# Sums over partitions as one marked float32 product, and page numbers read early, in a decoder-layer step

## The chip, the cores and the metric

The kernel runs on one core of a Trainium2 chip. The metric is the device time of one execution in microseconds; the number quoted for the kernel before is the median of three runs. One further execution was profiled, and all rows shown come from it.

## The reference

One layer of a decoder is applied to a prompt of 256 tokens and to eight samples of four tokens each, with the same float32 weights. Cut to what matters here:

```python
h = rms_norm(x, g_mix)
proj = h @ w_in                              # conv, q/k/v, memory q, three gates
u = u_lin * sigmoid(u_gate)                  # conv branch: causal depthwise conv, width 31
c = silu(layer_norm(depthwise(u), g_conv_ln, b_conv_ln));  y_conv = c @ w_conv_out
q = rms_norm(q_sb, g_q_sb);  k = rms_norm(k_sb, g_k_sb)    # 8 heads of 128
z = q . k / sqrt(128) + b_sb                 # stick-breaking attention, strictly causal
log_keep = where(causal, log_sigmoid(-z), 0)
after = reverse_cumsum(log_keep) - log_keep  # sum over the keys between s and t
a = where(causal, exp(log_sigmoid(z) + after), 0);  y_sb = (a @ v) @ w_sb_out
y_mem = softmax(rms_norm(q_mem) . k_mem / sqrt(128)) @ v_mem @ w_mem_out   # 256 memory tokens, 4 heads
x = x + (gA * y_conv + gB * y_sb + gM * y_mem) @ w_o
x = x + square(relu(rms_norm(x, g_mlp) @ w_up)) @ w_down
```

The samples also attend to a paged cache of 256 past tokens: `page_table` (8 samples x 2 pages) says which pages of `cache_sb_k` and `cache_sb_v` are theirs. New keys, values, convolution states and memory keys and values are outputs too.

## The kernel before

Activations lie with features on the 128 partitions and the 288 tokens (256 of the prompt, 32 of the samples) along the free dimension. All weights come from one array `wall` of 504 slabs of 128 x 1024 float32 (512 KB), in the order of their use; four slabs fit in the buffers `wr`.

Precision of the large products is kept by splitting. A cast on ScalarE (`cast_weights`, line 295) writes the part of a slab that the format float32r holds, `wh`; a subtraction on VectorE (`sub_part`, line 306) writes the rest, `wl`, and frees the slab buffer for the next load (line 278). Activations are split likewise into `h` and `l`. Each weight block of 128 x 128 then takes three products of 288 columns (`chunk`, line 465): high with high, high with low, low with high. A slab of eight blocks is 24 products.

Sums over the 128 partitions (of squares in the norms) are products with a matrix of ones. `total` (lines 429 and 430) makes them from an operand that was split first, with `ones_r`, a float32r copy of the ones: two products of 288 columns. It is called by `sum_norm` for the two norms over the model dimension, twice by `conv_norm`, and once in each of the 20 `head_norm`s (8 keys, 8 queries, 4 memory queries). In each stick-breaking head (`sb_head`) the sum over later keys is a product with a triangular matrix of zeros and ones: two products of 384 columns with `tri_r` (lines 1072 and 1074) on a split operand, and between them one of 128 columns with `ones` in plain float32 (line 1073). `mem_norm` (line 455) sums the memory's squares with four plain float32 products of one column. Other small products, such as scores (lines 843 and 1050) and transposes (lines 852 and 1036), are plain float32.

The order of instructions on each engine is written out at build time by the class `Order`. Each step of the work is a generator that yields `Ask(engine, us, flags, ...)`; the planner gives every step a price, keeps a clock for each engine and for the buffers, and places the step whose planned start comes first, with a rank for ties. Engines then run their queues in that order, waiting on semaphores. `MM` and `MM_MEM` are planned prices of products. The planner's `SP` is the SyncE queue, which issues nearly every transfer: slabs, `xT` and `memT`, stores, and tiles of the caches (`load_tiles`, nine buffers `k4`).

The 16 page numbers are loaded into `pt` early by one small transfer and read into SyncE registers inside `page_tiles` (line 927), when the first tile of cached keys is asked for; after that each tile is issued as two transfers (line 931). The planner counts 0.9 us for each tile and nothing more for the first. The four stages that use page tiles are the cached keys and then values of heads 0 to 3, and the same for heads 4 to 7; two stages before them use the memory caches through the same `load_tiles`.

In `sb_head`, after a head's value projection is scaled on VectorE (line 1031), PE transposes it (line 1036), and at the end of a head ScalarE and VectorE split its output (lines 1092 and 1094).

Of the kernel before, what the change touches and what calls it, by code (L numbers as in the profile page):

```python
# [7 lines left out]
F32 = mybir.dt.float32  # L8
# [6 lines left out]
P = 128  # L15
# [3 lines left out]
NB = 8  # L19
# [154 lines left out]
VISIT = 4  # L174
MM = 0.1325
MM_MEM = 0.226


@with_exitstack
def tile_decoder_step(ctx: ExitStack, tc: tile.TileContext, xT, memT, wall, cvec, kmat, ptab,  # L180
# [46 lines left out]
    nc.gpsimd.memset(eps, EPS)  # L227
    ones = cpool.tile([P, P], F32, name="ones")
    nc.gpsimd.memset(ones, 1.0)
    ones_r = cpool.tile([P, P], F32R, name="ones_r")  # L230
    nc.vector.tensor_copy(ones_r, ones)
# [10 lines left out]
    tri_r = cpool.tile([P, P], F32R, name="tri_r")  # L242
# [9 lines left out]

    def col(c):
        return cv[:, c:c + 1]

    def blocks2(x, n):

# [115 lines left out]
    def loads():  # L373

        xs = [(0, 3), (3, 6), (6, 9), (9, 12), (12, 15), (15, 16)]
        for k2 in range(KT // 2):
            yield sp(s=1)
            raw = tl("s", [P, 512]).rearrange("p (k t) -> p k t", k=2)
            here = [Flag(), Flag()]
            for i in range(2):  # L380
                if i:
                    yield sp()
                nc.sync.dma_start(raw[:, i], memT[:, 2 * k2 + i, :])
                here[i].at = order.landed(131)
                for s in (2 * k2, 2 * k2 + 1):
                    yield sp(**({} if i else {"wr": 1}))
                    load_slab(s, i)
                if i == 0:
                    add(prep_mem(k2, raw, here), 0.5 + 0.01 * k2)
            if k2 >= 1 and xs:  # L390
                k0, k1 = xs.pop(0)
                yield sp(k4=1)
                x = tl("k4", [P, 1024])[:, :(k1 - k0) * T].rearrange("p (k t) -> p k t", k=k1 - k0)
                nc.sync.dma_start(x, xT[:, k0:k1, :])
                there = Flag()
                there.at = order.landed(147 * (k1 - k0))
                for k in range(k0, k1):
                    add(prep_x(k, x[:, k - k0], there, k == k1 - 1), 1.5 + 0.01 * k)
            if k2 == 1:
                yield sp()  # L400
                nc.sync.dma_start(cv[:, C_BGATE:], cvec[:, C_BGATE:])
            if k2 == 2:
                yield sp()
                nc.sync.dma_start(km, kmat)
                km_in.at = order.landed(213)
                yield sp()
                nc.sync.dma_start(pt, ptab)
        for s in range(KT, N_SLABS):
            yield sp(wr=1)
            load_slab(s, 0)  # L410
# [12 lines left out]
        yield dve(n)  # L423
        nc.vector.scalar_tensor_tensor(out, a, 1.5, y, op0=ALU.add, op1=ALU.mult)

    def total(h, l, n):

        ss = bank("pa")[:, :n]
        nc.tensor.matmul(ss, ones_r, h, start=True, stop=False)  # L429
        nc.tensor.matmul(ss, ones_r, l, start=False, stop=True)  # L430
        return ss

    def sum_norm(acc, dim, out, flag, ready):

        yield act(T, ready, t=2)
        acc = acc[0]
        h, l = tl("t", [P, T], F32R), tl("t", [P, T], F32R)
        nc.scalar.copy(h, acc)
        yield dve(T)
        nc.vector.tensor_sub(l, acc, h.bitcast(F32))  # L440
        yield pe(2 * MM, pa=1)
        ss = total(h, l, T)
        yield from rsqrt_of(ss, T, dim, acc, tl("t", [P, T]), out)
        give("pa")
        give("t", 3)
        done(flag)

    rm_done, rx_done, r2_done = Flag(), Flag(), Flag()

    def mem_norm():  # L450
        yield pe(1.0, sums_m, pa=1)
        ss = bank("pa")[:, :MT]
        for m in range(MT):
            for i in range(2):
                nc.tensor.matmul(ss[:, m:m + 1], mem_sum[0][:, i * ML + m * P:i * ML + (m + 1) * P], ones[:, 0:1],
                                 start=(i == 0), stop=(i == 1))
# [233 lines left out]
    def conv_norm():  # L690

        yield dve(T, *conv_done, t=1)
        acc = tl("t", [P, T])
        nc.vector.tensor_add(acc, conv[0], conv[1])
        for j in (2, 3):
            yield dve(T)
            nc.vector.tensor_add(acc, acc, conv[j])
        for turn in range(2):
            yield act(T, t=1)
            h = tl("t", [P, T], F32R)  # L700
            nc.scalar.copy(h, acc)
            yield dve(T, t=1)
            l = tl("t", [P, T], F32R)
            nc.vector.tensor_sub(l, acc, h.bitcast(F32))
            yield pe(2 * MM, pa=1)
            ss = total(h, l, T)
            give("t", 2)
# [65 lines left out]

    def head_norm(ps, gcol, box, flag, p="pm"):

        yield dve(T, rx_done, t=4)
        raw, sq, h, l = (tl("t", [P, T], F32R if i > 1 else F32) for i in range(4))
        nc.vector.tensor_mul(raw, ps, rx)
        give(p)
        yield act(T)  # L780
        nc.scalar.activation(sq, raw, AF.Square)
        yield act(T)
        nc.scalar.copy(h, sq)
        yield dve(T)
        nc.vector.tensor_sub(l, sq, h.bitcast(F32))
        yield pe(2 * MM, pa=1)
        ss = total(h, l, T)
# [6 lines left out]
        give("t", 4)  # L794
        box.append(out)
        done(flag)

# [109 lines left out]

    def load_tiles(load, tiles, flags, which):
        for b in which:
            yield Ask("SP", 0.9, (), k4=1)  # L910
            t, kb = load(b)
            tiles.append(t)
            flags[b].at = order.landed(kb) + 1.0
# [5 lines left out]
            return t, 524  # L919
        return load  # L920

    pages = []

    def page_tiles(cache, g, spec):
        def load(b):
            if not pages:
                pages.extend(nc.sync.value_load(pt[0:1, i:i + 1], min_val=0, max_val=kpool.shape[0] - 1)
                             for i in range(2 * NB))
# [98 lines left out]
    def sb_head(h):  # L1027
        def evac(ps):
# [15 lines left out]
            give("pa")  # L1044
            give("a")
            done(v_made[h])
            yield pe(0.75, k_made[h], q_made[h], pa=1, s=4)
# [5 lines left out]
            z, l, sp_, hh = (tl("s", [P, 512], F32R if i == 3 else F32) for i in range(4))  # L1053
# [10 lines left out]
            nc.scalar.copy(hh[:, :384], ss)  # L1064
# [4 lines left out]
            nc.vector.tensor_sub(low, ss, hh[:, :384].bitcast(F32))  # L1069
            yield pe(0.6, pa=1)  # L1070
            af = bank("pa")[:, :384]
            nc.tensor.matmul(af, tri_r, hh[:, :384], start=True, stop=False)
            nc.tensor.matmul(af[:, 128:256], ones, sp_[:, 256:384], start=False, stop=False)
            nc.tensor.matmul(af, tri_r, low, start=False, stop=True)
            yield dve(384)
            nc.vector.tensor_sub(zz, zz, af)
            give("pa")
            give("s", 3)
            yield act(384)
            act_fn(LN_EXP, zz, zz, AF.Exp)  # L1080
            yield dve(256)
# [268 lines left out]
            give("a", 32)  # L1350

    def setup():
        yield dve(P, km_in)
        nc.vector.tensor_copy(tri_r, tri)
        yield pool(1)
        nc.gpsimd.memset(sb_s[:, T:T + 1], 0.0)

    with tc.manual_schedule():
# [165 lines left out]
```

## Time and profile before

| | |
|---|---|
| runs | 1669.57, 1672.0, 1673.81 us; median 1672.0 |
| profiled execution | 1670.29 us, span from first to last instruction 1668.3 us |
| PE (TensorE products) | busy 1661.0 us, 12778 records |
| DVE (VectorE) | busy 960.2 us, 1401 instructions |
| ACT (ScalarE) | busy 731.4 us, 1035 instructions |
| POOL (GpSimd) | busy 137.6 us |
| weight slabs | 488 loads of 512 KB and 32 of 256 KB |
| cache pages | 64 loads of 256 KB |

PEld is PE's loading of weights, which overlaps its products. SPq is SyncE's queue. Names of tiles are those of the program: `wr`, `wh`, `wl` are a raw slab, its high and its low part; `pm`, `pa`, `pl` are PSUM banks; `a`, `t`, `s` are activation tiles; `k` is a tile of a cache; `km` holds the constant matrices. Lnnn is a line of the kernel; a product in plain float32 can stand in the trace as more than one record.

### The profile page before, as it was taken

To read this page: it belongs to the slowest core of one execution; us is meant where nothing else is said; L and a number is where in the kernel's file an instruction comes from. 1 tells how busy PE (TensorE), PEld (TensorE's weight loads), DVE (VectorE), ACT (ScalarE), POOL (GpSimd) and SP (SyncE) were. 2 spreads that over 40 slices of the span, in tenths; PEclk is the share of its full clock that TensorE was granted. 3 is DMA by queue.
4 is the path that set the end of the run, shared out by engine and by line. 5 is a ranking of instruction groups with operands and counts; after the bars stand their busy time and mean duration, and the time that the engine had idled before them with its cause. 6 is when DMAs were issued, how large, how long until landed. Compare 5 with 4: busy or idle time off the path is not lost.

```text
span 1668.3 us, 30827 instructions
## 1 busy us (share of the span) xinstructions
PE 1661.0 (100%) x12778; PEld 1640.9 (98%) x12778; DVE 960.2 (58%) x1401; ACT 731.4 (44%) x1035; POOL 137.6 (8%) x105
## 2 busy tenths in 40 slices
PE   9999999999999999999999999999999999999999
PEld 7999998999999999999999999999999999999999
DVE  7887877776765555555555544455444554445443
ACT  8746655553463334444443333333333333333332
POOL 0020000000000000001222200122001210022100
PEclk9999999999999999999999999999999999999999
DMA  9686557756554555556655555555555555555553
GB/s 329 215 181 235 201 198 258 270 201 229 169 164 163 168 165 166 165 166 193 191 174 166 165 165 168 166 168 168 166 165 166 165 169 170 165 164 165 176 188 98
DMA packets 107103, 305.38 MB, mean 183 GB/s; under 512 B 19923, under 2 KB 29523, under 8 KB 106963
## 3 DMA queue, kind: packets, MB, share of 16 engines
q1 hardware_dynamic: 106818, 303.39, 57.3%
q8 instruction: 100, 1.64, 0.4%
q14 instruction: 41, 0.33, 0.1%
q10 hardware_dynamic: 144, 0.02, 0.0%
HBM read 297.05 MB, written 6.32 MB: 182 GB/s over the span
## 4 chain that ended last, share of the span: by engine, by line
PE 98%; DMA 1%; ACT 0%; SPq 0%; DVE 0%; issue 0%; ACTq 0%
PE pm L465 91%; PE pm L516 3%; PE pa L465 1%; PE pl L952 1%; DMA wr<-in_wall 1%; PE pl L1112 0%; DMA k<-in_kpool 0%; PE pl L968 0%; PE pa L1050 0%; PE pa L843 0%; PE pa L860 0%; PE pa L430 0%; PE pa L429 0%; PE pa L852 0%; PE pa L1051 0%; ACT wh L295 0%
## 5 line engine op out<-in xcount | busy, mean ns | idle before, releaser
L465 PE MATMUL pm<-a,wh 128*128 128x288 f32 x7744 | 1115.8, 295 | 0.0
L465 PEld LDWEIGHTS pm<-a,wh 128*128 128x128 f32 x7744 | 1054.4, 188 | 1.6 <-issue 1.4
L295 ACT CAST wh<-wr 128x1024 fp32r<-128x1024 f32 (+1 forms) x520 | 530.3, 1023 | 680.7 <-PE pm L465 621.5
L306 DVE TENSOR_TENSOR wl<-wr,wh 128x1024 fp32r<-128x1024 f32 (+1 forms) x520 | 618.3, 1192 | 213.4 <-ACT wh L295 210.9
L465 PE MATMUL pm<-a,wl 128*128 128x288 f32 x3872 | 600.6, 295 | 0.0
L465 PEld LDWEIGHTS pm<-a,wl 128*128 128x128 f32 x3872 | 542.8, 188 | 0.8 <-issue 0.6
L1249 POOL TENSOR_TENSOR t<-t 128x288 f32<-128x288 f32 x64 | 96.2, 1503 | 611.3 <-DVE t L1246 611.3
L1263 DVE TENSOR_TENSOR a<-a,pm 128x288 f32<-128x288 f32 x64 | 29.1, 454 | 127.0 <-PE pm L465 127.0
L1252 ACT CAST a<-t 128x288 fp32r<-128x288 f32 x64 | 27.7, 434 | 134.0 <-POOL t L1249 134.0
L1246 DVE SCALAR_TENSOR_TENSOR t<-pm,r 128x288 f32<-128x288 f32 x64 | 29.3, 458 | 96.6 <-PE pm L465 96.6
L1165 DVE TENSOR_TENSOR t<-pm,rx 128x288 f32<-128x288 f32 x48 | 22.0, 458 | 80.2 <-PE pm L465 80.2
L1254 DVE TENSOR_TENSOR a<-t,a 128x288 fp32r<-128x288 f32 x64 | 29.2, 458 | 63.4 <-ACT a L1252 63.4
L1235 POOL TENSOR_TENSOR t<-t,t 128x288 f32<-128x288 f32 x15 | 21.6, 1441 | 478.7 <-ACT t L1232 478.7
L683 DVE SCALAR_TENSOR_TENSOR a<-a,cv,a 128x256 f32<-128x256 f32 x120 | 57.9, 482 | 1.2
L516 PE MATMUL pm<-wh,a 128*128 128x512 f32 x128 | 35.9, 403 | 0.2 <-ACT wh L295 0.2
L516 PEld LDWEIGHTS pm<-wh,a 128*128 128x128 f32 x128 | 24.4, 192 | 6.6 <-ACT wh L295 1.2
L1184 DVE TENSOR_TENSOR t<-pm,t 128x288 f32<-128x288 f32 x32 | 14.7, 458 | 24.5 <-PE pm L465 17.6
L1220 DVE TENSOR_TENSOR a<-pm,t 128x288 f32<-128x288 f32 x16 | 7.3, 458 | 29.5 <-PE pm L465 29.5
L219 ACT ACTIVATE t<-pa,eps 128x288 f32<-128x288 f32 x23 | 11.5, 502 | 25.6 <-PE pa L430 25.6
L219 ACT ACTIVATE t<-t,cv 128x288 f32<-128x288 f32 x48 | 21.8, 524 | 0.0
L516 PE MATMUL pm<-wl,a 128*128 128x512 f32 x64 | 20.3, 399 | 0.0
L670 POOL TENSOR_TENSOR k<-a,cv 128x992 f32<-128x992 f32 x4 | 9.9, 2478 | 103.6 <-DVE a L656 103.6
(188 smaller groups left out, 579.2 us busy)
## 6 DMA issues: line engine op xcount, KB each, us to landing
wr<-in_wall SPq DMA_DIRECT2D x488, 512.0 KB, 3.6
wr<-in_wall SPq DMA_DIRECT2D x32, 256.0 KB, 4.8
k<-in_kpool SPq DMA_DIRECT2D x32, 256.0 KB, 5.7
k<-in_vpool SPq DMA_DIRECT2D x32, 256.0 KB, 5.7
k<-in_mkc SPq DMA_DIRECT2D x8, 512.0 KB, 8.4
k<-in_mvc SPq DMA_DIRECT2D x8, 512.0 KB, 5.9
t<-in_xT SPq DMA_DIRECT2D x16, 144.0 KB, 3.6
out_yT<-a SPq DMA_DIRECT2D x16, 144.0 KB, 1.8
```

The costliest lines, as they stand in the source:

```text
L219: nc.scalar.activation(out, src, func, **kw)
L295: nc.scalar.copy(sl.h[:, c], sl.raw[:, c])
L306: nc.vector.tensor_sub(sl.l[:, c], sl.raw[:, c], sl.h[:, c].bitcast(F32))
L465: nc.tensor.matmul(ps, w, a, start=(first and i == 0), stop=(last and i == len(todo) - 1))
L516: nc.tensor.matmul(ps[m], x[:, m * P:(m + 1) * P], y[:, w], start=(k == 0 and j < 2), stop=(k == KT - 1 and j in (4, 5)))
L683: nc.vector.scalar_tensor_tensor(c[:, :NP], up[:, k:k + NP], w, c[:, :NP], op0=ALU.mult, op1=ALU.add)
L1165: nc.vector.tensor_mul(g, ps, rx)
L1246: nc.vector.scalar_tensor_tensor(r, ps, 0.0, r2, op0=ALU.max, op1=ALU.mult)
L1249: nc.gpsimd.tensor_mul(r, r, r)
L1252: nc.scalar.copy(a.h, r)
L1254: nc.vector.tensor_sub(a.l, r, a.h.bitcast(F32))
L1263: nc.vector.tensor_add(x1[j], x1[j], ps)
```

## The change

A helper issues a float32 product with the attribute `is_weight_onezero` set. `total` uses it once on the unsplit operand, and the heads use it for the triangular and the ones matrix; the splits ahead of them, `ones_r` and `tri_r` go away. The memory norm adds the two halves of its sums on VectorE first and makes two plain products instead of four. The page numbers are read by a job of their own, `read_pages`, one at a time, with at least 2.5 us between planned reads, from 20 us after the planned landing of the table; every `load_tiles` waits for its end, and a tile is planned at 1.05 us. Prices in the plan follow, so the written order of all queues changes in the first part of the program.

```diff
+MM_01 = 0.245
...
+    def matmul_01(out, weights, x, start=True, stop=True):
+        pe_ = nc.tensor
+        pe_.add_instruction(mybir.InstMatmult(
+            name=nc.get_next_instruction_name(), start_tensor_calc=start, stop_tensor_calc=stop,
+            is_weight_onezero=True, tile_size=(P, P), tile_position=(0, 0),
+            ins=[pe_.lower_ap(x), pe_.lower_ap(weights, for_matmul_weights=True)], outs=[pe_.lower_ap(out)]))
...
                 nc.sync.dma_start(pt, ptab)
+                pt_in.at = order.landed(1) + 20.0
...
-    def total(h, l, n):
+    def total(x, n):
         ss = bank("pa")[:, :n]
-        nc.tensor.matmul(ss, ones_r, h, start=True, stop=False)
-        nc.tensor.matmul(ss, ones_r, l, start=False, stop=True)
+        matmul_01(ss, ones, x)
         return ss
...
     def mem_norm():
-        yield pe(1.0, sums_m, pa=1)
+        yield dve(ML, sums_m)
+        both = mem_sum[0][:, :ML]
+        nc.vector.tensor_add(both, both, mem_sum[0][:, ML:])
+        yield pe(0.5, pa=1)
         ss = bank("pa")[:, :MT]
         for m in range(MT):
-            for i in range(2):
-                nc.tensor.matmul(ss[:, m:m + 1], mem_sum[0][:, i * ML + m * P:i * ML + (m + 1) * P], ones[:, 0:1],
-                                 start=(i == 0), stop=(i == 1))
+            nc.tensor.matmul(ss[:, m:m + 1], both[:, m * P:(m + 1) * P], ones[:, 0:1], start=True, stop=True)
...
     def head_norm(ps, gcol, box, flag, p="pm"):
-        yield dve(T, rx_done, t=4)
-        raw, sq, h, l = (tl("t", [P, T], F32R if i > 1 else F32) for i in range(4))
+        yield dve(T, rx_done, t=3)
+        raw, sq = tl("t", [P, T]), tl("t", [P, T])
...
-        yield act(T)
-        nc.scalar.copy(h, sq)
-        yield dve(T)
-        nc.vector.tensor_sub(l, sq, h.bitcast(F32))
-        yield pe(2 * MM, pa=1)
-        ss = total(h, l, T)
+        yield pe(MM_01, pa=1)
+        ss = total(sq, T)
...
     def load_tiles(load, tiles, flags, which):
         for b in which:
-            yield Ask("SP", 0.9, (), k4=1)
+            yield Ask("SP", 1.05, (pages_in,), k4=1)
...
+    def read_pages():
+        for i in range(2 * NB):
+            yield Ask("SP", 0.6, (pt_in,), 2.5)
+            pages.append(nc.sync.value_load(pt[0:1, i:i + 1], min_val=0, max_val=kpool.shape[0] - 1))
+        done(pages_in)
...
         def load(b):
-            if not pages:
-                pages.extend(nc.sync.value_load(pt[0:1, i:i + 1], min_val=0, max_val=kpool.shape[0] - 1)
-                             for i in range(2 * NB))
             t = tl("k4", [P, 2, 4, P])
...
-            yield act(384)
-            nc.scalar.copy(hh[:, :384], ss)
...
-            yield dve(384)
-            low = tl("s", [P, 512], F32R)[:, :384]
-            nc.vector.tensor_sub(low, ss, hh[:, :384].bitcast(F32))
-            yield pe(0.6, pa=1)
+            yield pe(0.45, pa=1)
             af = bank("pa")[:, :384]
-            nc.tensor.matmul(af, tri_r, hh[:, :384], start=True, stop=False)
-            nc.tensor.matmul(af[:, 128:256], ones, sp_[:, 256:384], start=False, stop=False)
-            nc.tensor.matmul(af, tri_r, low, start=False, stop=True)
+            matmul_01(af, tri, ss, True, False)
+            matmul_01(af[:, 128:256], ones, sp_[:, 256:384], False, True)
...
+        add(read_pages(), 4.0)
```

`sum_norm` and `conv_norm` lose their splits in the same way as `head_norm`.

More of the change, by code (lines that the diff above doesn't have):

```diff
@@ L229, in tile_decoder_step @@
     nc.gpsimd.memset(ones, 1.0)
-    ones_r = cpool.tile([P, P], F32R, name="ones_r")
-    nc.vector.tensor_copy(ones_r, ones)
     ones_s = cpool.tile([P, T], F32, name="ones_s")
@@ L241, in tile_decoder_step @@
     snew = km[:, K_SNEW:K_SNEW + NS]
-    tri_r = cpool.tile([P, P], F32R, name="tri_r")
     rx = cpool.tile([P, T], F32, name="rx")
@@ L424, in rsqrt_of @@
         nc.vector.scalar_tensor_tensor(out, a, 1.5, y, op0=ALU.add, op1=ALU.mult)
-    def total(h, l, n):
+    def total(x, n):
         ss = bank("pa")[:, :n]
-        nc.tensor.matmul(ss, ones_r, h, start=True, stop=False)
-        nc.tensor.matmul(ss, ones_r, l, start=False, stop=True)
+        matmul_01(ss, ones, x)
         return ss
     def sum_norm(acc, dim, out, flag, ready):
-        yield act(T, ready, t=2)
+        yield pe(MM_01, ready, pa=1, t=1)
         acc = acc[0]
-        h, l = tl("t", [P, T], F32R), tl("t", [P, T], F32R)
-        nc.scalar.copy(h, acc)
-        yield dve(T)
-        nc.vector.tensor_sub(l, acc, h.bitcast(F32))
-        yield pe(2 * MM, pa=1)
-        ss = total(h, l, T)
+        ss = total(acc, T)
         yield from rsqrt_of(ss, T, dim, acc, tl("t", [P, T]), out)
         give("pa")
-        give("t", 3)
+        give("t", 2)
         done(flag)
@@ L698, in conv_norm @@
         for turn in range(2):
[L699 to L707, printed above, removed]
+            yield pe(MM_01, pa=1)
+            ss = total(acc, T)
             if turn == 0:
@@ L781, in head_norm @@
         nc.scalar.activation(sq, raw, AF.Square)
-        yield act(T)
[L783 to L787, printed above, removed]
+        yield pe(MM_01, pa=1)
+        ss = total(sq, T)
         r = tl("t", [P, T])
@@ L793, in head_norm @@
         nc.vector.scalar_tensor_tensor(out, raw, col(gcol), r, op0=ALU.mult, op1=ALU.mult)
-        give("t", 4)
+        give("t", 3)
         box.append(out)
@@ L920, in mem_tiles @@
         return load
-    pages = []
+    pages, pages_in, pt_in = [], Flag(), Flag()
+    def read_pages():
[3 more added lines that the diff above has]
+        done(pages_in)
     def page_tiles(cache, g, spec):
         def load(b):
-            if not pages:
-                pages.extend(nc.sync.value_load(pt[0:1, i:i + 1], min_val=0, max_val=kpool.shape[0] - 1)
-                             for i in range(2 * NB))
             t = tl("k4", [P, 2, 4, P])
@@ L1046, in evac @@
             done(v_made[h])
-            yield pe(0.75, k_made[h], q_made[h], pa=1, s=4)
+            yield pe(0.75, k_made[h], q_made[h], pa=1, s=3)
             k, q = ks[h][0], qs_[h][0]
@@ L1052, in evac @@
             give("a", 2)
-            z, l, sp_, hh = (tl("s", [P, 512], F32R if i == 3 else F32) for i in range(4))
+            z, l, sp_ = (tl("s", [P, 512]) for i in range(3))
             yield act(384)
@@ L1077, in evac @@
             give("pa")
-            give("s", 3)
+            give("s", 2)
             yield act(384)
@@ L1352, in setup @@
     def setup():
-        yield dve(P, km_in)
-        nc.vector.tensor_copy(tri_r, tri)
         yield pool(1)
```

## The prediction

> **What bounds the kernel now.** I began with the page: its span, the busy shares, and the chain that ended last.
>
> ```profile
> span 1668.3 us, 30827 instructions
> PE 1661.0 (100%) x12778; PEld 1640.9 (98%) x12778; DVE 960.2 (58%) x1401; ACT 731.4 (44%) x1035; POOL 137.6 (8%) x105
> PE 98%; DMA 1%; ACT 0%; SPq 0%; DVE 0%; issue 0%; ACTq 0%
> ```
>
> TensorE (PE) is busy for all but 7.3 us of the span, and VectorE and ScalarE have plenty of room. So an edit is worth what it takes off PE's own work, or off the few moments in which PE stands still. The next view, the waits of PE, lists those moments (who waited <- for whom: us in total, times, longest):
>
> ```profile
> PE pa L1036 <- DVE a L1031: 2.6, 1, 2.6
> PE pa L1312 <- POOL eps L227: 1.3, 1, 1.3
> PE pm L516 <- ACT wh L295: 0.2, 1, 0.2
> ```
>
> The 1.3 us is the start of the program. Only one real hole is left, 2.6 us long, at a transpose in a stick-breaking head. The stretches around it (from:to, its length, then busy us and count of PE, PEld, DVE, ACT and POOL, granted clock, share of the DMA engines, GB/s) show what came before it:
>
> ```profile
> 230.00:235.00 5.00, 5.00 (x40) 5.00 (x39) 3.39 (x8) 2.48 (x6) 0.00 (x0) 1.00 0.36 118
> 235.00:240.00 5.00, 5.00 (x40) 4.93 (x39) 3.41 (x7) 2.42 (x5) 0.00 (x0) 1.00 0.02 3
> 255.00:258.00 3.00, 2.55 (x20) 2.32 (x18) 1.81 (x5) 0.11 (x1) 0.00 (x0) 1.00 1.04 399
> 258.00:260.00 2.00, 0.00 (x0) 0.00 (x0) 0.76 (x3) 1.32 (x3) 0.00 (x0) 1.00 1.05 413
> ```
>
> Twenty microseconds before PE stops, the DMA engines move almost nothing (3 GB/s); when PE stops they are full. The instructions of the page-table line say why nothing moved (duration min/median/max in ns, first and last start in us):
>
> ```profile
> L927 SPq TENSOR_LOAD <-pt x16: 262/262/492, 231.0 to 239.8; - x16
> L927 SPq FUSED_REGOPS  x16: 147/147/178, 231.6 to 240.1; - x16
> L927 SPq SEQ_ASSERT  x16: 18/18/28, 231.8 to 240.3; - x16
> ```
>
> SyncE (SP) issues nearly every transfer, and from 231.0 to 240.3 it does nothing but read the 16 page numbers: 9.3 us, or 0.58 us for each. The timeline gives what follows from that (start, length, instruction, count, and in brackets the idle time before it and what ended it):
>
> ```profile
> 227.14 3.83 SPq L278 DMA_DIRECT2D wr<-in_wall  x2
> ...
> 242.51 0.37 SPq L278 DMA_DIRECT2D wr<-in_wall  x1
> ...
> 251.27 0.34 SPq L278 DMA_DIRECT2D wr<-in_wall  x1
> ...
> 257.89 1.04 ACT L295 CAST wh<-wr 128x1024 fp32r<-128x1024 f32 x1 [3.27 <-DMA wr<-in_wall]
> 258.84 0.37 ACT L1092 CAST a<-pa 128x256 fp32r<-128x256 f32 x1
> ...
> 259.24 0.42 DVE L1094 TENSOR_TENSOR a<-pa,a 128x256 fp32r<-128x256 f32 x1 [2.33 <-ACT a L1092]
> 259.58 0.45 DVE L1031 TENSOR_TENSOR a<-pm,rx 128x288 f32<-128x288 f32 x1
> ...
> 260.17 0.30 PE L1036 MATMUL pa<-km,a 128*128 128x128 f32 x1 [2.62 <-DVE a L1031]
> ```
>
> No weight slab is issued from 230.97 to 242.51. Then slabs and cache pages crowd the DMA engines, and the slab issued at 251.27 reaches its cast only at 257.89. ScalarE stood at that cast for 3.27 us although PE would need the slab much later; behind it in the same queue was the small L1092, behind that on VectorE L1094 and L1031, and PE's next instruction in order was the transpose of L1031's result. A late transfer became a PE hole through the order of two queues.
>
> **The page reads.** The edit takes the 16 reads out of that place and puts them into SP's queue one by one: the first stands after the issue of slab 17, the last after that of slab 34. A slab is 24 products, so by the steady price of a product below (0.1325 us) that is one read in about 3.4 us. They pass the stores of the memory values and keys and the first conv history loads. With 0.58 us each they cost SP the same 9.3 us, and nothing else is issued by them. What they hold up is the slab issue behind them. Two rows price that:
>
> ```profile
> SPq L278 <- DVE wl L306: 1210.5, 452, 9.6
> L295 ACT CAST wh<-wr 128x1024 fp32r<-128x1024 f32 (+1 forms) x520 | 530.3, 1023 | 680.7 <-PE pm L465 621.5
> ```
>
> SP waits 1210.5 us for VectorE to free slab buffers, 2.7 us each time, so a 0.58 us read mostly replaces waiting; and the casts wait for PE (621.5 of 680.7 us), not for transfers. I take zero. If that cover were gone everywhere, the cost would be at most 9.3 us; no row points there, and I leave that end outside the range. The new condition that tile loads wait for all reads (the memory tiles too) holds nothing: their first issue stands ten slabs after the last read.
>
> At the old place the DMA hole goes, so I credit the whole 2.6 us. What could be late next is a slab behind the page transfers themselves. Other stretches with such bursts, around the memory keys, both value reads and the second key read:
>
> ```profile
> 133.00:143.00 10.00, 10.00 (x81) 9.46 (x83) 8.02 (x18) 5.78 (x11) 0.00 (x0) 1.00 0.98 386
> 281.00:291.00 10.00, 10.00 (x78) 9.93 (x77) 7.94 (x21) 5.63 (x11) 0.00 (x0) 1.00 0.95 327
> 330.00:340.00 10.00, 10.00 (x77) 9.93 (x77) 7.54 (x15) 5.42 (x10) 0.00 (x0) 1.00 1.04 402
> 375.00:390.00 15.00, 15.00 (x169) 14.41 (x168) 10.06 (x23) 4.27 (x5) 0.00 (x0) 1.00 0.97 369
> ```
>
> The DMA engines are as full there, and PE never stops. The burst alone doesn't make the hole; the burst after a pause does.
>
> **The products with ones and zeros.** From the chain, in order of time (start, length, piece):
>
> ```profile
> 46.49 0.79 PE pa L455 x8
> 125.53 0.86 PE pa L843 x4
> 174.00 0.17 PE pa L1072
> 174.17 0.22 PE pa L1073 x2
> 174.39 0.18 PE pa L1074
> 174.57 0.14 PE pa L429
> 174.71 0.13 PE pa L430
> 175.64 0.44 PE pa L852 x4
> 462.70 398.31 PE pm L465 x3006
> ```
>
> A main product of 288 columns takes 398.31/3006 = 0.1325 us, and the two halves of a total (L429, L430) take twice that, 0.265. A plain float32 product stands as two records, each with a weight load: L843 is two products of 256 columns in four records, 0.215 us a record, or 0.84 ns for a column in each. A marked product appears nowhere in this trace, so its price is bounded: from above by both records (288 columns: 0.484 us), from below by one main product (0.1325 us). I take one record, 0.242 us, because weights of 0 and 1 leave nothing for a second part of the weights, and because the transposes (L852, four products in four records), whose other operand is zeros and ones too, cost 0.11 us for 128 columns, the same 0.86 ns a column.
>
> [...]
>
> Sum at one record: 24 totals (two norms, two in the conv norm, 20 head norms) x (0.265 - 0.242) = 0.55 us. Eight stick-breaking heads: now 0.17 + 0.22 + 0.18 = 0.57; then 384 columns 0.32 + 128 columns 0.11 = 0.43; 8 x 0.14 = 1.1. Memory norm: eight records 0.79 become four, 0.4 saved. Together 2.05 us, all on PE.
>
> **The operand splits.** They go from ScalarE and VectorE:
>
> ```profile
> L783 ACT CAST t<-t 128x288 fp32r<-128x288 f32 x20 | 8.7, 434 | 0.5
> L785 DVE TENSOR_TENSOR t<-t,t 128x288 fp32r<-128x288 f32 x20 | 9.0, 452 | 0.8 <-ACT t L783 0.8
> L1064 ACT CAST s<-s 128x384 fp32r<-128x384 f32 x8 | 4.1, 508 | 0.2
> L1069 DVE TENSOR_TENSOR s<-s,s 128x384 fp32r<-128x384 f32 x8 | 4.4, 552 | 0.0
> ```
>
> That is 12.8 us of ScalarE and 13.4 of VectorE here, a little more with the four other totals and the two weight copies; one addition of 256 columns comes back on VectorE for the memory norm. I price all of it at zero, because PE waits for neither engine but in the one hole. The hand-made plan also reorders: products that follow a total come earlier, and fewer buffers are held. With queues this full of PE work that moves nothing unless it makes a new hole.
>
> **Sum.** 2.6 + 2.05 = 4.7 us. The profiled execution took 1670.3 (span 1668.3 and 2.0 around it): it would take 1665.6. The median of the three runs before is 1.7 above the profiled one, and they spread over 4.2 us; from the median the sum is 1667.3. PE's steady stream can hardly vary, the hole can, so part of the spread may belong to what goes. I take the middle of the two, 1666.5, and for the rivals the like.
>
> **The rivals.** B, the mark saves no pass: each total costs 0.484 - 0.265 = 0.22 more, each head 0.645 + 0.22 - 0.57 = 0.295 more, so 5.3 + 2.4 - 0.4 - 2.6 = 4.6 us slower, 1675.8 from 1674.9 and 1676.6. Against it stand the one-record transposes; for it, that no row shows the mark. It decides from about 1.3 ns a column.
>
> C, the hole stays or reappears at one other place in the new order: only 2.05 us are won, 1669.1. For it: the key pages still come with the slabs and ScalarE's queue still lets a late slab hold small steps.
>
> D, the other side: the pages are now asked for earlier and each of the four page bursts, not one, puts a late slab at the head of ScalarE's queue, 2.6 us each. Four holes for one are 7.9 us more, less 2.05: 5.8 slower, 1677.0. It undoes the gain from the second hole on. For it: DMA at 399 to 413 GB/s while PE stood. Against it: the four stretches above.
>
> E, the mark takes one main-rate pass: 24 x 0.1325 + 8 x (0.57 - 0.23) + 0.4 + 2.6 = 8.9 us won (0.23: L1072's 0.17 and a third of it), 1662.2.
>
> **The numbers.** Forecast 0.64, C 0.15, D 0.08, B 0.08, E 0.05. About 0.3%, 5.0 us, is what a measurement of this kernel can tell from no change, so faster begins at 1667.0, in the middle of my forecast's span. I count 0.48 of the forecast and E as faster, 0.53; the other 0.16, C and half of B as same, 0.35; D and half of B as slower, 0.12. The range must hold the forecast, C (up to 1669.9, and 2 us more for the spread between runs) and half of E: 1662 to 1672.
>
> **What would show it.** Right: the PE waits list nothing over 0.5 us after the start; the page reads lie singly and long before 231 us, and no stretch near 235 falls to a few GB/s; each total is one record of about 0.24 us and a head's two products take about 0.43. Wrong: totals in two records (B); a PE wait near 250 or at another page burst with a slab's cast ahead of it (C, D); casts that wait for transfers between the first and the last read, if the reads aren't covered.

## The result and the profile after

| | before | after |
|---|---|---|
| median of 8 runs each | 1671.38 us (1669.57 to 1673.81) | 1676.24 us (1676.05 to 1676.45) |
| ratio after/before, 95% interval | | 1.003 [1.0019, 1.0041] |
| profiled execution | 1670.29 us, span 1668.3 | 1676.45 us, span 1674.7 |

The changed kernel is 0.3% slower. The forecast was 1666.5 us, and the range ended at 1672. The likeliest case failed and rival B, in which the mark saves nothing, gave 1675.8. The page of the kernel after, its span and busy times:

```profile
span 1674.7 us, 30765 instructions
PE 1669.8 (100%) x12774; PEld 1644.7 (98%) x12774; DVE 951.3 (57%) x1368; ACT 716.9 (43%) x1001; POOL 138.7 (8%) x105
```

PE is busy 8.8 us longer (1669.8 for 1661.0) and stands still less. The waits of PE after the change hold only the start:

```profile
PE pa L1302 <- POOL eps L228: 1.3, 1, 1.3
PE pm L519 <- ACT wh L302: 0.3, 1, 0.3
```

The hole is gone. So is the pause of the transfers, in the stretches of the kernel after:

```profile
235.00:240.00 5.00, 5.00 (x41) 4.99 (x40) 4.49 (x9) 2.45 (x4) 0.00 (x0) 1.00 0.79 285
255.00:260.00 5.00, 5.00 (x61) 4.30 (x63) 4.11 (x9) 2.59 (x5) 0.48 (x1) 1.00 0.65 210
```

285 GB/s stand where 3 stood, and PE is busy for all of 255 to 260. The line of the page numbers in the kernel after:

```profile
L920 SPq TENSOR_LOAD <-pt x16: 262/273/637, 40.6 to 90.8; - x16
```

What the marked products cost is in the chain of the kernel after (start, length, piece), a total at 72.94 and a head at 200.05, and in its groups by shape (count, then busy us and mean ns of one, which overlap each other):

```profile
72.94 0.48 PE pa L258 x2
...
197.96 0.49 PE pa L258 x2
...
200.05 0.87 PE pa L258 x4
```

```profile
L258 PE MATMUL pa<-t,ones 128*128 128x288 f32 x48 | 15.8, 409 | 0.0
L258 PE MATMUL pa<-s,km 128*128 128x384 f32 x16 | 6.5, 486 | 0.0
L258 PE MATMUL pa<-s,ones 128*128 128x128 f32 x16 | 3.1, 274 | 0.0
```

24 totals stand as 48 records, and 16 products of the heads as 32. A marked product has two records like the other plain float32 products here, the transposes apart. A total takes 0.485 us instead of 0.265 and a head's products 0.87 instead of 0.57. That is 24 x 0.22 + 8 x 0.30 = 7.7 us more; with the hole (2.6) and the memory norm (0.4) off, 4.7. To see where the time goes, the main products (the 11,712 of `chunk`) are numbered from 0, and the end of each is taken from the trace. At the end of main product 3000 the kernel after is 4.63 us behind (516.76 against 512.13 us from the span's start), at the last one 6.4. Of the other 1.8 us, 0.2 is the one total that comes behind product 3000; the rest comes in 8700 main products that were not changed. The chains of the long steady stretch, of the kernel before and then after:

```profile
861.29 788.72 PE pm L465 x5965
```

```profile
460.94 402.60 PE pm L468 x3042
...
864.02 786.05 PE pm L468 x5928
```

With the row of 3006 products that the prediction shows, this is 1187.03/8971 = 132.32 ns for a product before and 1188.65/8970 = 132.51 after. A difference of 0.2 ns is nothing for one product, and some 1.6 us for 8700.

### The profile page after: what moved, and what is told of

Same layout as the page of the kernel before. It is cut to its first block, busy times and chain, and to the rows that moved or that the text cites. A ratio compares the mean times of both kernels' runs of the same rounds, so it can differ in the third digit from the quotient of the medians.

```text
span 1674.7 us, 30765 instructions
## 1 busy us (share of the span) xinstructions
PE 1669.8 (100%) x12774; PEld 1644.7 (98%) x12774; DVE 951.3 (57%) x1368; ACT 716.9 (43%) x1001; POOL 138.7 (8%) x105
## 4 chain that ended last, share of the span: by engine, by line
PE 99%; DMA 0%; SPq 0%; ACT 0%; DVE 0%; issue 0%
PE pm L468 92%; PE pm L519 3%; PE pa L258 1%; PE pa L468 1%; PE pl L948 1%; PE pl L1102 0%; DMA wr<-in_wall 0%; PE pl L964 0%; PE pa L852 0%; PE pa L835 0%; PE pa L1046 0%; PE pa L1077 0%; PE pa L1076 0%; PE pa L1047 0%; PE pa L1075 0%; PE pa L844 0%
## 5 line engine op out<-in xcount | busy, mean ns | idle before, releaser
L686 DVE SCALAR_TENSOR_TENSOR a<-a,cv,a 128x256 f32<-128x256 f32 x120 | 61.5, 512 | 0.9
L220 ACT ACTIVATE s<-s 128x384 f32<-128x384 f32 (+1 forms) x30 | 15.2, 509 | 6.5 <-DVE s L1066 5.9
```

The source lines that it names most:

```text
L220: nc.scalar.activation(out, src, func, **kw)
L686: nc.vector.scalar_tensor_tensor(c[:, :NP], up[:, k:k + NP], w, c[:, :NP], op0=ALU.mult, op1=ALU.add)
```

## The experiments

Three questions were open: whether the mark does anything, what made the hole, and where the loss of the steady stretch comes from. A version of the program is called a build. The planner writes the order of every version anew.

**The mark taken off** (the kernel after in everything else):

```diff
-            is_weight_onezero=True, tile_size=(P, P), tile_position=(0, 0),
+            is_weight_onezero=False, tile_size=(P, P), tile_position=(0, 0),
```

> The changed kernel with the attribute set to false in all its marked products; nothing else differs. Theory M (the mark changes no pass): each total still stands as two records and takes 0.485 us, the two products of a head 0.87 us, and the time is that of the changed kernel, 1676.2 us, to 1 us. Rival F (the mark saves something and the loss came from elsewhere): unmarked products are dearer than the marked ones by up to a record of 0.24 us for each total, so up to 8 us slower, 1677 to 1684.

Measured: 1676.23 us (1676.05 to 1676.53), 1.0033 [1.0021, 1.0044] of before, against 1676.24 with the mark. Its chain:

```profile
197.67 0.49 PE pa L258 x2
199.76 0.87 PE pa L258 x4
```

The same prices to 0.01 us: the mark changes nothing in time. Whether the attribute reaches the engine at all, no trace shows. Nor does this yet say why a transpose has one record.

**The transposes as plain products** (in the kernel after): the eight transposes of the memory keys become float32 products with the identity, and the sixteen of the memory heads the same with the mark on the moving operand.

```diff
+    def matmul_id(out, weights, x):
...
+            is_fmap_onezero=True, tile_size=(P, P), tile_position=(0, 0),
...
-                    nc.tensor.transpose(tp[:, i * ML + m * P:i * ML + (m + 1) * P], raw[m][:, h * HD:(h + 1) * HD], ident)
+                    nc.tensor.matmul(tp[:, i * ML + m * P:i * ML + (m + 1) * P], raw[m][:, h * HD:(h + 1) * HD], ident, start=True, stop=True)
...
-                    nc.tensor.transpose(tp[:, m * NP + a * P:m * NP + (a + 1) * P],
-                                        p[:, a * ML + m * P:a * ML + (m + 1) * P], ident)
+                    matmul_id(tp[:, m * NP + a * P:m * NP + (a + 1) * P],
+                              p[:, a * ML + m * P:a * ML + (m + 1) * P], ident)
```

> The changed kernel, with 8 transposes of memory keys issued as plain float32 products with the identity, and 16 of the memory heads as such products with the moving operand marked as zeros and ones. Theory T (the transposes' single record belongs to the transpose operation, not to their zeros and ones, and no mark takes a pass away): 16 and 32 records, 0.22 us for each product of 128 columns, 24 x 0.11 = 2.6 us more in all. Rival F2 (a mark on the moving operand counts, or a product with the identity is recognized): one record and 0.11 us for the marked 16.

Measured in one run: 1679.43 us. The groups by shape of these transposes in the kernel after (L844 of the memory heads, L604 of the memory keys), and of the products in their place, marked (L265) and unmarked (L611):

```profile
L844 PE MATMUL pa<-km,s 128*128 128x128 f32 x16 | 2.4, 272 | 0.0
L604 PE MATMUL pa<-km,s 128*128 128x128 f32 x8 | 1.2, 272 | 0.0
...
L265 PE MATMUL pa<-km,s 128*128 128x128 f32 x32 | 4.2, 274 | 0.0
L611 PE MATMUL pa<-km,s 128*128 128x128 f32 x16 | 2.1, 274 | 0.0
```

24 products with the same operands as the transposes stand as 48 records instead of 24. The last main product ends 3.3 us later than in the version without the mark, 0.5 of it from the start; 24 x 0.11 = 2.6 was the price by count. The single record belongs to the transpose as an operation. Zeros and ones in an operand are not what makes it cheap, with or without a mark.

**The page reads alone**, early and spread, in the kernel before:

```diff
-            yield Ask("SP", 0.9, (), k4=1)
+            yield Ask("SP", 1.05, (pages_in,), k4=1)
...
+        add(read_pages(), 4.0)
```

> The kernel before with the early, spread page reads alone; products and memory norm as before. Theory M: the hole of 2.6 us goes and nothing comes in its place, 1668.8 us against 1671.4, and no PE wait over 0.5 us after the start. Rival C (a hole somewhere else in the new order): a PE wait of 1 us or more at another place, 1670 to 1672. Rival S (the price of the steady products moves with the order): no hole, but the mean of a main product after 500 us differs from the kernel before by 0.1 to 0.4 ns or more, which is 1 to 4 us either way.

Measured: 1669.71 us (1669.61 to 1670.05), 0.9994 [0.9985, 1.0003] of before; profiled 1669.75, span 1667.6. Its waits of PE and its steady chain:

```profile
PE pa L1317 <- POOL eps L227: 1.3, 1, 1.3
PE pm L517 <- ACT wh L295: 0.3, 1, 0.3
```

```profile
460.88 398.51 PE pm L466 x2999
859.65 790.37 PE pm L466 x5970
```

The hole goes and nothing takes its place. While the 16 reads pass, they cost nothing: main product 1300 ends at 255.01 us, before at 255.05. Product 1600 ends 2.83 us earlier than before. Then 1188.88/8969 = 132.55 ns for a steady product, against 132.32, gives back 2.0 of it; 0.7 is left at the end. Here is a loss like that of the kernel after, in a kernel with the old products.

**The products alone**: the kernel after with the late reads of before.

```diff
-            yield Ask("SP", 1.05, (pages_in,), k4=1)
+            yield Ask("SP", 0.9, (), k4=1)
...
-        add(read_pages(), 4.0)
+            if not pages:
+                pages.extend(nc.sync.value_load(pt[0:1, i:i + 1], min_val=0, max_val=kpool.shape[0] - 1)
+                             for i in range(2 * NB))
```

> The changed kernel with the page reads put back to the first tile of keys (16 together, tile price 0.9 as before); marked products and the shorter memory norm stay. Theory M: 24 x 0.22 + 8 x 0.30 - 0.4 = 7.3 us slower than the kernel before with a hole like before's, 1678.7 us. Rival C: the new order has no hole even with the late reads, 1676.1, and the early reads won nothing by themselves.

Measured: 1677.02 us (1676.86 to 1677.51), 1.0038 [1.0024, 1.0051]. Its one wait of PE after the start, and its stretches at the pause and at the burst:

```profile
PE pa L1070 <- DVE s L1067: 0.2, 1, 0.2
```

```profile
235.00:240.00 5.00, 5.00 (x41) 4.99 (x40) 4.49 (x9) 2.73 (x5) 0.00 (x0) 1.00 0.00 0
250.00:255.00 5.00, 4.99 (x38) 4.76 (x37) 4.12 (x9) 3.00 (x7) 0.00 (x0) 1.00 1.04 405
```

The transfers stop (0 GB/s) and the burst follows (405), but the only wait is 0.2 us. So a pause and a burst do not make the hole by themselves. The timelines of ScalarE and PE show that a late slab does not either:

```profile
257.29 1.05 ACT L302 CAST wh<-wr 128x1024 fp32r<-128x1024 f32 x1 [2.22 <-DMA wr<-in_wall]
258.24 0.36 ACT L1077 CAST a<-pa 128x256 fp32r<-128x256 f32 x1
...
259.01 3.64 PE L1097 MATMUL pl<-k,k 128*32 128x256 f32 x64
262.65 0.33 PE L1027 MATMUL pa<-km,a 128*128 128x128 f32 x1
```

A cast waits 2.22 us for its slab with a head's small cast behind it, as in the kernel before. But PE has 64 products with cached keys (L1097) to do ahead of the transpose (L1027, the L1036 of before). In the kernel before these products stand behind the transposes:

```profile
260.71 3.64 PE L1112 MATMUL pl<-k,k 128*32 128x256 f32 x64
```

By the medians the early reads are worth about 0.8 us in this order; only 0.3 of it stands at product 3000 (517.05 against 516.76 us), the rest comes in the steady stretch.

**The late reads told to the plan**: in the kernel before, the reads stay together and late, and the plan counts their 9.3 us.

```diff
                 pages.extend(nc.sync.value_load(pt[0:1, i:i + 1], min_val=0, max_val=kpool.shape[0] - 1)
                              for i in range(2 * NB))
+                order.free["SP"] += 9.3
+                order.now.ready += 9.3
```

> The kernel before with its 16 reads left together at the first tile of keys, but with 9.3 us counted for them in the plan, so that every queue's written order allows for the pause. Theory P (a pause that the plan doesn't know of makes the hole): no PE wait over 0.5 us after the start, and the 1600th main product ends 2.6 us earlier than in the kernel before, apart from the start. Rival Q (the pause itself makes it, since no slab is issued for 9 us): a PE wait of 2 us or more remains near 250 us.

Measured: 1669.79 us (1669.46 to 1669.91), 0.9993 [0.9983, 1.0002]; span 1667.7. Its stretches, and then its timeline of SyncE and of ScalarE (as in the prediction):

```profile
235.00:240.00 5.00, 5.00 (x40) 4.93 (x39) 3.41 (x7) 2.42 (x5) 0.00 (x0) 1.00 0.02 3
...
255.00:258.00 3.00, 3.00 (x25) 3.00 (x24) 2.93 (x7) 1.20 (x2) 0.00 (x0) 1.00 1.06 380
```

```profile
241.45 4.06 SPq L278 DMA_DIRECT2D wr<-in_wall  x4
245.70 7.67 SPq L933 DMA_DIRECT2D k<-in_kpool  x12
```

```profile
253.60 0.37 ACT L1094 CAST a<-pa 128x256 fp32r<-128x256 f32 x1 [0.48 <-PE pa L1089]
253.87 1.05 ACT L295 CAST wh<-wr 128x1024 fp32r<-128x1024 f32 x1
```

The pause is the same (3 GB/s), the burst is much the same (380 GB/s for 399), and PE is busy throughout. The order differs: after the pause four slabs go out ahead of the next twelve page halves, where the kernel before alternated one slab and four to six halves, and the head's small cast (L1094 here, L1092 before) stands ahead of the slab's cast instead of behind it. So counting the 9.3 us of SyncE is enough to close the hole, by another order of several queues; which of the moves closes it, no run separates. The expected 2.6 us do not stand at product 1600, which ends 7.6 us earlier than before because other work now comes behind it, but at product 2000 (2.5 us).

**The kernel before once more, twice**, for its spread of some 4 us: 

> The kernel before, unchanged, with a profile of its own. Its runs spread over 4.2 us, those of the changed kernel over 0.4. Theory W (the spread is in the hole): the PE wait at the head's transpose differs from 2.6 us by as much as the time differs from 1670.3. Theory S (the spread is in the steady part): the wait is 2.6 us to 0.3, and the mean main product after 500 us differs from the first profile's.

> The kernel before, unchanged, profiled a third time, for its spread of some 4 us, which none of the versions without the 2.6 us hole shows (0.4 to 1.1 us). Of the two profiled executions so far one ended its first main product at 51.70 us and had a hole of 2.6 us, the other ended it at 53.98 us, with a granted clock of 0.56 from 9 to 12 us, and had a hole of 2.1 us; from product 3000 on they agree to 0.1 us. Theory St (the spread is the start): the third execution's span is 1668.3 us plus what its first main product ends after 51.70 us, within 0.6 us, whatever the hole. Rival H (the spread is the hole): the first product ends at 51.7 us or so, and the span goes with the length of the hole, which then lies outside 2.1 to 2.6 us.

Measured: 1670.73 us (1669.31 to 1672.98) and 1672.37 us (1669.83 to 1672.80); profiled spans 1670.1 and 1670.5 for 1668.3. From product 3000 on the three profiled executions agree to 0.1 us. Waits of PE in the second execution and stretches of PE at its start (length, busy us and count, granted clock, DMA share, GB/s):

```profile
PE pa L1036 <- DVE a L1031: 2.1, 1, 2.1
PE pm L516 <- ACT wh L295: 1.8, 1, 1.8
```

```profile
9.00:12.00 3.00, 3.00 (x9) 0.56 0.98 352
```

And in the third, its hole and the stretches of PE behind it:

```profile
PE pa L1036 <- DVE a L1031: 2.7, 1, 2.7
```

```profile
258.00:261.00 3.00, 0.34 (x3) 0.95 1.06 417
261.00:264.00 3.00, 3.00 (x35) 0.50 0.99 359
264.00:267.00 3.00, 3.00 (x51) 0.98 0.79 245
```

The first execution, with a hole of 2.6 us, in the same stretch:

```profile
261.00:264.00 3.00, 3.00 (x64) 1.00 0.94 329
```

After a wait the granted clock fell to about a half for some 3 us, once at the start (0.56 in that stretch) and once behind the hole (0.50); behind the holes of 2.6 and 2.1 us in the first two executions it stayed at 1.00. The second execution had lost 2.28 us at product 0 and kept that until the hole; the third lost 0.54 at the start and 1.63 more between products 1300 and 1600. Neither expectation for the third holds: its span is 1.6 us above what its start explains, and the hole hardly varies in length (2.1 to 2.7 us). What varies is the price of the products behind it. The two falls followed waits of 1.8 and 2.7 us; what decides whether the clock falls after a wait, no run shows.

The mean granted clock of every run, to a thousandth, is on record as well, and it says what most of the spread is. Of 102 runs of the kernel before, timed beside these versions, 47 had a clock of 1.000 and spans of 1667.2 to 1669.1 us, 52 had 0.999 and 1669.1 to 1671.1, and three had 0.998 and 1671.6 to 1672.5. A thousandth of 1670 us is 1.7 us, an estimate of what each step costs; the medians of the first two groups are 1669.99 and 1671.82 us. All 86 runs of the versions without a hole had 1.000, and those of one version spread over 0.4 to 1.1 us. So most of the kernel before's spread goes with its clock, and the clock falls in the kernel with the hole. Where in a run it fell is known for the profiled executions only: behind the hole in one, at the start in another.

**What a steady product's price hangs on.** Two versions of "page reads alone" leave the order and shift something else: one warm-up product more, and 128 bytes of padding ahead of all buffers.

```diff
-        for i in range(7):
+        for i in range(8):
```

```diff
+    pad = cpool.tile([P, 32], F32, name="pad")
+    nc.gpsimd.memset(pad[:, 0:1], 0.0)
```

> The kernel with the early page reads alone, and one more warm-up product at the start (8 for 7): all buffers' addresses and the order stay, only PE's instruction stream is shifted by one product. Theory I (the place in the instruction stream sets the price of the steady products): the products of 148 ns move to other places or go, and the mean per 480 products changes by over 0.2 ns in several stretches. Theory B (the buffers' addresses set it): the means stay to 0.05 ns in every stretch.

> The kernel with the early page reads alone, and 128 bytes of padding ahead of the pools: the order stays, every buffer lies 128 bytes further. Theory B (the buffers' addresses set the price of the steady products): the mean per 480 products changes by over 0.2 ns in several stretches, 1 to 3 us in all, either way. Theory I (the instruction stream sets it): the means stay to 0.05 ns.

Measured: 1669.99 us (1669.38 to 1670.32) and 1670.09 us (1669.64 to 1670.51). The mean price of a product, taken over nine stretches of 960, is that of "page reads alone" to 0.01 ns in every stretch. Neither one warm-up product more nor a shift of all buffers by 128 bytes matters. The third version changes which activation buffers follow each other, and nothing in PE's order:

```diff
+        yield pe(0.0, a=1)
+        nc.gpsimd.memset(tl("a", [P, T])[:, 0:1], 0.0)
+        give("a")
```

> The kernel before with the page numbers read early and spread, and one more activation tile that is allocated, gets one column set by GpSimd and is freed again just ahead of the output projection (about 230 us). The order of PE's instructions, all weight blocks and all PSUM banks stay as in that version without the tile; only the buffers that later activation tiles get are rotated. By count of the built program the buffer is the same in all 960 main products from number 2928, in 954 of the 960 after them, in 675, 495, 425, 692, 355, 565 and 609 of the following stretches of 960. The version without the tile has there, as mean time per product, 132.49, 132.58, 133.84, 132.18, 132.21, 132.69, 132.40, 132.43 and 132.45 ns. Theory A (the price of a steady product goes with the activation buffers that follow each other): the first two stretches stay to 0.05 ns, and most of the other seven move by 0.1 ns or more, up to 1.4 ns in the third (133.84); the last product moves by some tenths of a us to 2 us. Rival O (the price goes with the order and timing of the instructions, not with the buffers): all nine stay to 0.05 ns.

Measured: 1670.64 us (1670.36 to 1670.86), 1.0 [0.999, 1.001]. The nine means are 132.49, 132.59, 134.31, 132.61, 132.56, 132.38, 132.50, 132.59 and 132.37 ns: the first two, with the same buffers, stay to 0.01, the next four move by 0.3 to 0.5, the last three by 0.1 to 0.2. (The third stretch holds a total as well, which adds 0.3 ns to its mean in each version.) The span grows by 1.2 us, of which 1.1 lie behind product 3000. Two stretches of PE show it (busy us and count), rotated first, then page reads alone, then the kernel before:

```profile
765.00:892.00 127.00, 126.90 (x949) 126.79 (x948) 1.00 0.59 178
892.00:1019.00 127.00, 127.00 (x960) 127.00 (x959) 1.00 0.55 166
```

```profile
765.00:892.00 127.00, 126.90 (x952) 126.79 (x951) 1.00 0.57 178
892.00:1019.00 127.00, 127.00 (x963) 127.00 (x962) 1.00 0.54 167
```

```profile
765.00:892.00 127.00, 126.89 (x959) 126.79 (x958) 1.00 0.58 181
892.00:1019.00 127.00, 127.00 (x963) 127.00 (x962) 1.00 0.53 166
```

PE is busy for all of it in each, at the full clock, and does 949, 952 or 959 products. So which activation buffers are used moves the price, by up to 0.5 ns here and with the instructions otherwise the same. Whether it is the single buffer or two that follow each other, which cost more, and why, stays open. That the kernel after has its loss in the steady stretch by this cause is the likeliest reading: its buffers differ too, but it was not tried on that kernel.

**What the prices point to**: without the marked products, the reads early and the memory norm with two products. The second version also makes the heads' `ones` product in two float32r parts:

```diff
-            for i in range(2):
-                nc.tensor.matmul(ss[:, m:m + 1], mem_sum[0][:, i * ML + m * P:i * ML + (m + 1) * P], ones[:, 0:1],
-                                 start=(i == 0), stop=(i == 1))
+            nc.tensor.matmul(ss[:, m:m + 1], both[:, m * P:(m + 1) * P], ones[:, 0:1], start=True, stop=True)
...
-            nc.tensor.matmul(af[:, 128:256], ones, sp_[:, 256:384], start=False, stop=False)
+            nc.tensor.matmul(af[:, 128:256], ones_r, hh[:, 256:384], start=False, stop=False)
+            nc.tensor.matmul(af[:, 128:256], ones_r, low[:, 256:384], start=False, stop=False)
```

> The kernel before with the page numbers read early and spread and the memory norm with two products instead of four; the totals and the heads as before. Theory M: 2.6 + 0.4 = 3.0 us below the kernel before, and 0.8 us above the version with the heads' ones product in two float32r parts. Rival L (price of steady products by build): between 1 and 5 us below the kernel before, and either side of the other version.

> What the measured prices point to: the kernel before with the page numbers read early and spread, the memory norm with two products instead of four, and in each of the eight stick-breaking heads the product of 128 columns with the ones matrix as two products in float32r on the two parts that are there already, instead of one plain float32 product. The marked products are left out. Theory M (only records and columns count): 2.6 us for the hole, 0.4 for the memory norm, and 8 x (0.22 - 2 x 0.06) = 0.8 for the heads, 3.8 us below the kernel before; the head's three pieces take about 0.46 us together. Rival L (the steady products of each build have a price of their own, within 0.2 ns of 132.5 ns over 11,700 products, so up to 2 us either way): anything between 1.8 and 5.8 us below, so 1665 to 1669 beside 1671. If the small products wait for their weight loads, two of 128 columns take 0.2 us and the heads win nothing: 3.0 us below.

Measured: 1668.04 us (1667.62 to 1668.47), 0.9981 [0.9972, 0.9990], and 1667.97 us (1667.51 to 1668.58), 0.9982 [0.9973, 0.9991]. Both beat both kernels, and the heads' parts win nothing. A head in the chain of the second version:

```profile
200.22 0.17 PE pa L1078
200.40 0.06 PE pa L1079
200.46 0.11 PE pa L1080
200.57 0.22 PE pa L1081
```

0.56 us, against 0.57 before: one of the small products comes at 0.06 us, and the next two pieces are longer by what that saved. The steady chain of the first version:

```profile
460.88 398.38 PE pm L467 x3003
859.53 790.56 PE pm L467 x5981
```

1188.94/8984 = 132.34 ns, the price of the kernel before. Its lead on "page reads alone", 1.7 us by the medians and 1.4 at the last product, is this price: at product 3000 it is 0.55 us behind that version, in the 8700 products after it gains 1.95. The memory norm's saving stands in the chain (0.34 us for 0.79) but not in the ends of the products there: product 0 ends 0.09 us earlier. Where the rest went was not followed.

## Why the prediction was right or wrong

**The marked product: wrong, and this decided the sign.** The step that failed is "I take one record, 0.242 us". It put the transposes' one record down to an operand of zeros and ones; the transposes written as plain products show that it is the operation. Each marked product stood as two records, 0.485 us for a total and 0.87 for a head's two, marked or not. Instead of 2.05 us won, the totals and heads lost 24 x 0.22 + 8 x 0.30 = 7.7 us and the memory norm gave 0.4 back in the chain. That is rival B's term to 0.1 us, and it had 0.08. Of its two bounds, the upper one was in a row of the same operation (a plain float32 product with `ones`, L1073, in two records), while the lower reading came from another operation. A marked total, 0.485 us for 288 columns, is 3.7 times a main product of 0.1325 us. That the second record belongs to "a second part of the weights" was the author's reading, and no trace shows what it does: in the kernel after, the 48 records of the totals have 48 weight loads of 188 ns (L258, median), although all the weights are ones.

**The hole: right in size for a run at the full clock, half right in cause.** 2.6 us were credited, 2.8 came off. What the sum did not have is the lower clock that goes with the hole in 55 of 102 runs, an estimated 1.7 us in most of them. "The burst after a pause does [make the hole]" is not enough: two versions have both and no hole. In the kernel before, a head's small cast stood behind a late slab's cast, and PE's next instruction needed a VectorE step (L1031) that stood behind the one waiting for the small cast (L1094). Each of the two versions lacks one of these: in one the small cast goes ahead, in the other PE has other work first. Rivals C and D did not come: the waits of PE list no other hole.

**The reads hidden: right.** With the page reads alone, product 1300 ends where it did, and between 38 and 92 us the casts of the kernel after wait for PE (9.5 us) and not for transfers.

**The splits at zero: right.** ScalarE and VectorE lose 14.5 and 8.9 us of busy time, and without them the terms as measured give the 4.63 us at product 3000 to 0.2 us (7.5 us of products up to there, 2.8 for the hole, and product 0 ends 0.16 us earlier).

**"PE's steady stream can hardly vary": wrong between builds.** Over the three profiled executions of the kernel before it agrees to 0.1 us. Between builds it moved by 0.2 ns for a product, up to 2 us in all. The sum had no term for it. The kernel before could not give its size, but the same stretches of 960 in its own trace, those with main products alone, range from 132.02 to 132.77 ns: the price was not one number there either. With it rival B's 4.6 us would have been 6.4. From the medians the loss is only 4.9, since the profiled execution of before lies 1.1 us under its median: in that execution the clock was full, and in 55 of 102 runs it was not. Against the median of before at a clock of 1.000, 1669.99 us, the kernel after loses some 6.2.

**"Part of the spread may belong to what goes": right.** It went from 4.2 us to 0.4, and the clocks of the runs show why.

## What to carry to other kernels

Price a new form of an instruction from the nearest row of the same operation, and take a cheaper row of another operation only after one run of that form alone. Where an order is written from planned times, work that the plan does not count can make a hole far from its own place, some 20 us behind it here; counting it closed the hole here as well as moving it did. A hole can cost more than its length, some 1.6 us more here where the granted clock fell to 0.50 behind it: look at the granted clock of every run, and not of the profiled one alone. In a kernel that is one steady stream on PE, an edit to the start can move the stream's own price by as much as the edit is worth (here by 2.0 us where the early reads had won 2.83, and by 1.95 where the memory norm was worth 0.4): compare where a fixed product ends before and behind the edit, not the total alone.

## What was not expected of the hardware

The price of a float32r product of 288 columns in a PE stream without gaps at the full clock goes with the activation buffers: 134.31 ns against 133.84 as the mean of the same 960 products (one total among them) in two builds that differ in them alone. Over three executions of the kernel before it is the same to 0.01 ns (0.1 us in some 8700 products). And a wait of 1.8 us in one execution and one of 2.7 us in another were followed by some 3 us at a granted clock of 0.56 and 0.50, waits of 2.6 and 2.1 us by none (1.00); over a whole run, 55 of 102 runs of the kernel with the hole had less than the full clock, and none of 86 without it.
